# A hybrid decoder layer on one core: the recurrence's output gate goes through the Strassen pass of the mixer gates, masked copies and scans are merged, and on-chip rows are padded to 4352 bytes

## The chip, the core and the metric

The kernel runs on one core of a Trainium2 chip. A core has a matrix engine (PE, with its weight loads listed as PEld), a vector engine (DVE), a scalar engine (ACT), a general engine (POOL), and SP, whose queue issues most of the DMA transfers. Each engine works through its own queue in order, and waits on semaphores for the others. Data lives in SBUF, where a tile has 128 partitions and a row of bytes in each, and matrix products are accumulated in PSUM, which has eight banks of 512 float32 columns per partition. The metric is the device time of one execution in microseconds (us). Lower is better.

## What is computed

One layer (DEPTH is 1) on 1024 tokens of width 1024, with 16 learned meta tokens in front, so 1040 positions:

```python
u = rmsnorm(h, mix_norm_pre[l])
proj = u @ w_in[l]
q, f_logit, i_in, g_out, v_pool, gate_a, gate_b = jnp.split(proj, cuts, axis=-1)
a = hgrn2(q, f_logit, i_in, g_out, lbs[l], hgrn_out_norm[l])
p = multiscale_pool(v_pool, pool_proj[l], pool_scale[l])
z = (jax.nn.sigmoid(gate_a.astype(jnp.float32)) * (a @ w_branch_hgrn[l])
     + jax.nn.sigmoid(gate_b.astype(jnp.float32)) * (p @ w_branch_pool[l]))
h = h + rmsnorm(z @ w_out[l], mix_norm_post[l])
...
# in hgrn2: a gated recurrence over chunks with 4 heads of 128, then
o = o * lax.rsqrt(jnp.mean(o * o, axis=-1, keepdims=True) + EPS)
o = o.reshape(bsz, L, HGRN_WIDTH) * out_gain.astype(jnp.float32)
return o * jax.nn.sigmoid(g.astype(jnp.float32))
...
# in a chunk of the recurrence
b = jnp.cumsum(lf, axis=2)
scores = jnp.einsum('bhtk,bhtsk,bhsk->bhts', q, decay, k)     # causal, decay = exp(b_t - b_s)
```

After it comes a gated MLP of width 2816 with a causal convolution of three taps on the gate. Columns of `w_in`: q, f, i and the output gate g are 512 wide each (four blocks of 128, one for each head), the pooled values 512, the mixer gates a and b 1024 each.

## The kernel before, in words

Every float32 product is made of three matmuls of a rounded type: an operand is split into a high part and the rest (`act.copy` makes hi, a subtraction makes lo), and hi x hi, hi x lo and lo x hi are added up. Features lie on partitions and tokens along the rows. The normalized input is kept as `uhi` and `ulo`, eight feature blocks of 1040 columns each.

**Stages.** (1) Rows are loaded, normalized and transposed, and nine tiles of the values i are computed (L1037). Meanwhile DVE and ACT make the sums of quarters of u (t1 to t4, `gate_steps`, L966) that a Strassen product needs; `SUMS_AT` says after which tile which step of them comes. (2) Two of the four output gate projections, G0 and G1, are done by `proj` (L175): 8 feature blocks, 3 chunks of 342 columns, 3 matmuls each, 72 in all. Their sigmoid is stored to DRAM (`post_g`, L779) and loaded again by the head that needs it (L750). (3) The mixer gates a and b, 16 blocks, are eight units of `Strassen` (L191), two blocks a unit: seven products (P1 to P7) of half the depth and half the tokens in place of eight. A product has 4 blocks x 3 matmuls of 512 columns, or twice as many of 258 and 256. The first EARLY = 4 units do P1 and P2, which need no sums, ahead of the rest (L1077), and leave P1 in a slot. Weights are loaded by `load_first` and `load_unit`, summed on POOL (L255 to L258), and split four products ahead (`ahead`, L211). `put_gate` (L838) adds the products, takes the sigmoid and stores the gate to DRAM. (4) The heads of the recurrence and the pooling, in the order of the string ORDER (L45): F, Q, G and PV are projections (forget gate, query, output gate, pooled values), `h` is the next step of a head (`head_steps`, L612), `c` the logarithms and the running sum of a forget gate (`chain_f`, L592), PP the pooling products, `sp` and `sa` splits, BB and BA the two branch products, `w` the preparation of MLP weights. G2 stands after the second h2, G3 before w0. G2 and G3 keep their sigmoid in a slot. (5) The output product, the MLP (Strassen again) and its down product.

**What sets the order.** In stages 1 to 3 the order on PE, ACT and DVE is written by hand (`manual_schedule`, L1002, up to the early products). In stage 4 a planner with its own costs places the instructions; PE's order follows ORDER closely. PSUM banks come from a pool of eight (`bank`, L95) and are taken in turn, so a new product waits until the tile eight banks before it has been read. SBUF tiles called slots (`slot`, L89) come from a pool of 24, of 1040 columns (4160 bytes) each. POOLED lists the operations of stage 4 that run on POOL in place of DVE.

**A head.** For six levels of block size (2 to 64), `level_in` (L623) makes decayed q and k on DVE, ACT and POOL, `level_mm` (L637) multiplies them on PE into a bank (`sl`), and `level_out` (L657) copies the wanted half of each block into the score tile `sc`: for levels under 32 by eight masked copies of 64 columns (L669), one for each chunk of 128 tokens. Diagonal blocks (`sb`) are copied by eight masked copies of 128 columns (L725). The running sum b of the logarithms is nine scans (L602), since it starts again at every chunk. Then come the transposes of k (`pt`), the states (`ds`, `st`), the output (`po`), its norm (`ms`, `rs`), and the multiplication with the sigmoid of g (L774).

## Time and profile before

| what | value |
|---|---|
| median of three runs | 1367.71 us (1365.0 to 1373.99) |
| the profiled execution | 1363.17 us, span 1361.5 us |
| mean granted PE clock | 0.997 |
| PE busy | 98% of the span |
| DVE busy | 70% |
| ACT busy | 42% |
| POOL busy | 32% |
| DMA | 236.68 MB, mean 174 GB/s |

How to read the profile. The span runs from the first to the last instruction, and busy time is what an engine spent in instructions. Matmuls are pipelined: the duration of one holds the time to fill and drain the array, so the next one starts before it ends, and the busy time of a group is the time that is covered by at least one. A row of the waits names the waiting engine and line, the one that ended the wait, and the total, the count and the longest. A row of a stretch has from:to, the length, then the busy time and the count of instructions for PE, PEld, DVE, ACT and POOL (an engine without any is left out where one tile was asked for), and at the end the granted clock, the DMA share and GB/s. A row of a timeline has the start, the time taken, the engine, the line, the operation, output and inputs, shapes and the count, and in brackets the idle time ahead of it with what ended it. A row of groups has shapes and count, then busy time and mean ns of one, then idle time before it.

### The profile page before, as it was taken

What the parts mean: (1) busy time and instruction counts of PE and PEld (TensorE: products, weight loads), DVE (VectorE), ACT (ScalarE), POOL (GpSimd) and SP (SyncE); (2) the same over time, 40 slices, a digit from 0 to 9 for tenths busy, and PEclk for the clock granted to TensorE, in tenths of its full rate; (3) what the DMA queues carried; (4) which work ended last, traced back from release to release, by engine and by line L of the source; (5) the groups of instructions that cost most, each with busy time, mean ns of one, the idle gap of its engine ahead of it and who ended that gap; (6) DMA issues with size and microseconds to landing.
All of it is one profiled execution on the core that took longest, in us unless ns stands there. A gap on an engine that the chain in (4) does not pass through costs nothing. (4 is left out here: it accounts for less than half of the span.)

```text
span 1361.5 us, 20285 instructions
## 1 busy us (share of the span) xinstructions
PE 1336.0 (98%) x7737; PEld 1181.8 (87%) x7737; DVE 952.4 (70%) x1414; ACT 565.9 (42%) x946; POOL 439.2 (32%) x326
## 2 busy tenths in 40 slices
PE   8999999999999999999999999999999999999997
PEld 7799899999999899987778888888888887888786
DVE  6754644388886768665568888888878776744557
ACT  6543333367455474225654222222222223543343
POOL 2015421237444600051021655454566742000100
PEclk9999999999999999999999999999999999999999
DMA  7134333311110158999876877756677799965624
GB/s 266 44 115 146 117 116 108 101 54 41 34 49 19 34 173 278 323 283 310 289 259 238 225 204 201 201 173 169 158 180 157 173 243 273 386 207 186 186 62 170
DMA packets 141455, 236.68 MB, mean 174 GB/s; under 512 B 9254, under 2 KB 77450, under 8 KB 141358
## 3 DMA queue, kind: packets, MB, share of 16 engines
q1 hardware_dynamic: 129294, 211.00, 46.2%
q0 software_dynamic: 12064, 24.38, 10.6%
q8 instruction: 61, 1.00, 0.3%
q14 instruction: 36, 0.29, 0.1%
HBM read 171.85 MB, written 86.53 MB: 190 GB/s over the span
## 5 line engine op out<-in xcount | busy, mean ns | idle before, releaser
L284 PE MATMUL P<-v,whi 128*128 128x512 f32 (+2 forms) x408 | 141.5, 354 | 2.1 <-ACT p L1486 1.2
L285 PE MATMUL P<-v,whi 128*128 128x512 f32 (+2 forms) x408 | 141.0, 353 | 0.0
L287 PE MATMUL P<-v,wlo 128*128 128x512 f32 (+2 forms) x424 | 135.6, 350 | 0.0
L172 PE MATMUL pd<-rot 128*128 128x512 f32 x272 | 106.0, 390 | 0.3 <-DVE rot L1413 0.3
L173 PE MATMUL pd<-rot 128*128 128x512 f32 x272 | 106.0, 390 | 0.0
L138 POOL TENSOR_TENSOR wlo<-wraw,whi 128x1024 fp32r<-128x1024 f32 (+1 forms) x19 | 45.8, 2415 | 164.6 <-ACT whi L137 94.8
L1413 DVE TENSOR_TENSOR rot<-yt,rot 128x1024 fp32r<-128x1024 f32 x33 | 41.2, 1250 | 71.6 <-ACT rot L1412 71.6
L284 PEld LDWEIGHTS P<-v,whi 128*128 128x128 f32 x408 | 76.8, 188 | 13.1 <-ACT p L1486 1.4
L229 ACT CAST whi<-wraw 128x512 fp32r<-128x512 f32 x78 | 46.1, 618 | 97.7 <-PE P L285 86.9
L285 PEld LDWEIGHTS P<-v,whi 128*128 128x128 f32 x408 | 76.9, 189 | 10.6
L287 PEld LDWEIGHTS P<-v,wlo 128*128 128x128 f32 x424 | 74.2, 188 | 11.0
L1301 POOL TENSOR_TENSOR ys<-y 128x512 f32<-128x512 f32 x22 | 35.3, 1603 | 139.6 <-issue 95.9
L230 DVE TENSOR_TENSOR wlo<-wraw,whi 128x512 fp32r<-128x512 f32 x74 | 65.4, 905 | 19.9 <-ACT whi L229 19.9
L171 PE MATMUL pd<-rot 128*128 128x512 f32 x272 | 72.8, 391 | 2.1 <-ACT rot L1412 1.2
L255 POOL TENSOR_TENSOR swa<-wraw,wraw 128x512 f32<-128x512 f32 x28 | 44.5, 1589 | 90.7 <-DMA wraw<-in_w_in_dram 60.7
L1412 ACT CAST rot<-yt 128x1024 fp32r<-128x1024 f32 x33 | 34.6, 1051 | 90.1 <-PE pd L172 90.1
L229 ACT CAST whi<-swa 128x512 fp32r<-128x512 f32 x56 | 33.4, 618 | 88.0 <-PE P L285 79.3
L137 ACT CAST whi<-wraw 128x1024 fp32r<-128x1024 f32 (+1 forms) x28 | 26.4, 943 | 100.3 <-PE ppv L185 19.6
L1345 DVE SCALAR_TENSOR_TENSOR y<-g,par,y 128x1024 f32<-128x1024 f32 x44 | 64.3, 1462 | 0.8
L171 PEld LDWEIGHTS pd<-rot 128*128 128x128 f32 x272 | 50.9, 188 | 13.7 <-ACT rot L1412 2.0
L229 ACT CAST whi<-swb 128x512 fp32r<-128x512 f32 x56 | 33.4, 619 | 67.2 <-PE P L285 63.1
L172 PEld LDWEIGHTS pd<-rot 128*128 128x128 f32 x272 | 51.1, 188 | 11.3 <-DVE rot L1413 0.7
(387 smaller groups left out, 4187.2 us busy)
## 6 DMA issues: line engine op xcount, KB each, us to landing
wraw<-in_w_in_dram SPq DMA_DIRECT2D x36, 512.0 KB
yt<-ysum SPq DMA_DIRECT2D x33, 512.0 KB
wraw<-in_ffn_w_gate_dram SPq DMA_DIRECT2D x26, 512.0 KB
wraw<-in_w_out_dram SPq DMA_DIRECT2D x24, 512.0 KB
wraw<-in_ffn_w_up_dram SPq DMA_DIRECT2D x22, 512.0 KB
wsum<-in_ffn_w_down_dram SPq DMA_DIRECT2D x22, 512.0 KB
ysum<-ys SPq DMA_DIRECT2D x11, 768.0 KB
sa<-sscr SPq DMA_DIRECT2D x16, 513.0 KB
```

Of the source, the lines that this page charges most:

```text
L138: eng.tensor_tensor(lo, raw, rr(hi), ALU.subtract)
L171: pe.matmul(ps, ahi, bhi, start=first, stop=False)
L172: pe.matmul(ps, ahi, blo, start=False, stop=False)
L173: pe.matmul(ps, alo, bhi, start=False, stop=last)
L229: act.copy(hi, src)
L230: (pool_e if 4 <= i < 2 * self.early else dve).tensor_tensor(lo, src, rr(hi), ALU.subtract)
L255: pool_e.tensor_tensor(s1, a21, a22, ALU.add)
L284: pe.matmul(d, whi[:, k, :], xh[:, c : c + w], start=(k == 0 and onto is None), stop=False, **go)
L285: pe.matmul(d, whi[:, k, :], xl[:, c : c + w], start=False, stop=False, **go)
L287: pe.matmul(x[:, o : o + w], wlo[:, k, :], xh[:, c : c + w], start=False, stop=(k == 3), **go)
L1345: dve.scalar_tensor_tensor(a, g[:, j : j + SEQ], cvw[:, j, m : m + 1], a, ALU.mult, ALU.add)
L1413: dve.tensor_tensor(lo, src, rr(hi), ALU.subtract)
```

## The change

- The projections G are no longer done by `proj`. The four blocks of g become two more units of the gates' Strassen object (ten units in place of eight), so all four sigmoids are stored by `put_gate` and every head loads its own. G2 and G3 leave ORDER, and the code of G0, G1 and `post_g` goes.
- P1 and P2 are done early for eight units in place of four. The sums' steps are placed after tiles 5 to 8 and then after single early products. The first loads of weights are placed anew.
- `level_out` copies a level (below 32) with one masked copy of 512 columns, its mask broadcast over the chunks. The diagonal blocks take two of 512 in place of eight of 128.
- The nine scans of a head become one over 1040 columns, which multiplies the running value by a tile `keep_on` (0 at the start of each chunk, else 1) and adds. The tile is made on POOL and holds one slot.
- Slots and feature rows are 1088 columns (4352 bytes). The features begin at column 48 of their row, and the MLP's quarters use rows of 544 columns. There are 26 slots. To make room, the scratch of software-issued DMA is set to 2048 bytes, `junk` becomes a slot, and the pool of small tiles is opened after that of the slots.

```diff
-EARLY_G = 2
-SUMS_AT = {5: (2,), 6: (2, 1), 8: (3,), 9: (1, 3), 10: (1, 4), 11: (4, 0), 12: (0, 0)}
-FM_SLOTS = 24
+EARLY_G = 8
+SUMS_AT = {5: (2,), 6: (2, 1), 8: (3,), 9: (1, 3), 10: (1,), 11: (4,), 12: (4,), 13: (0,), 14: (0,), 15: (0,)}
+FM_SLOTS = 26
+LP = 1088
+U0 = LP - L
...
-        return stage["fm", "p"].tile([P, n], dtype, tag="fm", name=nm(name), padded_shape=[P, L])
+        return stage["fm", "p"].tile([P, n], dtype, tag="fm", name=nm(name), padded_shape=[P, LP])
...
-        for t0, rows in row_tiles:
-            dve.tensor_tensor_scan(b[:, t0 : t0 + rows], f[:, t0 : t0 + rows], f[:, t0 : t0 + rows],
-                                   0.0, ALU.add, ALU.bypass)
+        dve.tensor_tensor_scan(b, keep_on, f, 0.0, ALU.mult, ALU.add)
...
-            m3 = masks[lv].rearrange("p (b h) -> p b h", h=lv)
-            for c in range(NCH):
-                dve.copy_predicated(o4[:, c], m3, p4[:, c])
+            m4 = masks[lv].rearrange("p (o b h) -> p o b h", o=1, h=lv).to_broadcast([P, NCH, nb, lv])
+            dve.copy_predicated(o4, m4, p4)
...
-            for i in range(4):
-                c = 4 * j + i
-                dve.copy_predicated(sc[:, c * P : (c + 1) * P], mbase, ps[:, i * P : (i + 1) * P])
+            dve.copy_predicated(sc[:, j * 512 : (j + 1) * 512].rearrange("p (c t) -> p c t", c=4),
+                                mbase.rearrange("p (o t) -> p o t", o=1).to_broadcast([P, 4, P]),
+                                ps.rearrange("p (c t) -> p c t", c=4))
...
-        if h < EARLY_G:
-            sgs[h] = slot(TQ, name="sg")
-            nc.sync.dma_start(sgs[h], sgd[h])
+        sg = slot(TQ, name="sg")
+        nc.sync.dma_start(sg, sd[2 * KD + h])
...
-    gates = Strassen([(WIN, c + 2 * P * j) for c in (CA, CB) for j in range(KD // 2)], range(KD), EARLY, gq,
+    gate_units = [(WIN, c + 2 * P * j) for c, n in ((CA, KD), (CB, KD), (CG, HEADS)) for j in range(n // 2)]
+    gates = Strassen(gate_units, range(len(gate_units)), EARLY_G, gq,
                      lambda u: True, put_gate, lambda u, i: None)
...
-        for e in range(0, EARLY, 2):
+        at = len(vtiles)
+        for e in range(0, EARLY_G, 2):
+            for i in (e + 3, e + 4):
+                if i < EARLY_G:
+                    gates.load_first(i)
             p = gates.start_pair(e)
             for f in [f[i] for i in range(2) for f in p]:
                 f()
-                for j in SUMS_AT.get(13, ()) if e == 0 else ():
+                for j in SUMS_AT.get(at, ()):
                     next(sums[j], None)
+                at += 1
...
-            fq[q] = [t[:, i * 4 * n : (i + 1) * 4 * n].rearrange("p (k t) -> p k t", k=4)]
+            fq[q] = [t[:, i, :, :n] if n == HT else t[:, i, :, :].rearrange("p k t -> p (k t)")[:, : 4 * n].rearrange("p (k t) -> p k t", k=4)]
...
-    nc = _bacc.Bacc("TRN2", target_bir_lowering=False, num_devices=1)
+    nc = _bacc.Bacc("TRN2", target_bir_lowering=False, num_devices=1, dynamic_dma_scratch_size=2048)
```

More of the change, by code (lines that the diff above doesn't have):

```diff
@@ L43 @@
 AHEAD = 3
-ORDER = ("F0 c0 Q0 h0 F1 h0 c1 Q1 h0 h1 F2 h1 c2 h0 Q2 h1 h2 G2 h0 h1 h2 h0 F3 h0 h2 c3 PV0 h1 h2 h1 Q3 h3 h1 h3 h1 "
-         "PV1 h3 sp0 PV2 h2 h3 sa1 sp1 sp2 PP0 h2 PV3 h2 h3 sp3 PP1 h0 G3 w0 h3 PP2 h3 PP3 w1 BB0 w4 h2 BB1 w4 BB2 "
+ORDER = ("F0 c0 Q0 h0 F1 h0 c1 Q1 h0 h1 F2 h1 c2 h0 Q2 h1 h2 h0 h1 h2 h0 F3 h0 h2 c3 PV0 h1 h2 h1 Q3 h3 h1 h3 h1 "
+         "PV1 h3 sp0 PV2 h2 h3 sa1 sp1 sp2 PP0 h2 PV3 h2 h3 sp3 PP1 h0 w0 h3 PP2 h3 PP3 w1 BB0 w4 h2 BB1 w4 BB2 "
          "w4 sa2 BB3 w5 h3 BB4 w5 BB5 w5 sa0 sa3 BA0 w5 BA1 w2 BB6 w3 BA2 BB7 BA3 BA4 BA5 BA6 BA7")
@@ L68, in trunk_kernel @@
     wst = ctx.enter_context(tc.tile_pool(name="wst", bufs=3))
-    sm = ctx.enter_context(tc.tile_pool(name="sm", bufs=4))
     PSUM = bass.MemoryType.PSUM
@@ L89, in slot, with ubig @@
     def slot(n, dtype=F32, name="s"):
-        return stage["fm", "p"].tile([P, n], dtype, tag="fm", name=nm(name), padded_shape=[P, L])
-    def ubig(dtype, name, n=KD * L):
-        return upool.tile([P, n], dtype, tag="u", name=nm(name), padded_shape=[P, KD * L])
+        return stage["fm", "p"].tile([P, n], dtype, tag="fm", name=nm(name), padded_shape=[P, LP])
+    def ubig(dtype, name, n=KD * LP):
+        return upool.tile([P, n], dtype, tag="u", name=nm(name), padded_shape=[P, KD * LP])
     def bank(name="ps"):
@@ L114, in trunk_kernel @@
     open_pool("fm", FM_SLOTS)
+    stage["sm"] = ExitStack()
+    sm = stage["sm"].enter_context(tc.tile_pool(name="sm", bufs=4))
     open_pool("ps", 8, PSUM)
@@ L413, in trunk_kernel @@
     uhi_f, ulo_f = ubig(F32R, "uhi"), ubig(F32R, "ulo")
-    uhi = uhi_f.rearrange("p (k t) -> p k t", k=KD)
-    ulo = ulo_f.rearrange("p (k t) -> p k t", k=KD)
+    uhi, ulo = (u.rearrange("p (k t) -> p k t", k=KD)[:, :, U0:] for u in (uhi_f, ulo_f))
     WIN = w_in[0]
@@ L569, in u_all @@
         return uhi[:, k, lo : lo + n], ulo[:, k, lo : lo + n]
-    def u_q(k, lo, n):
-        return uhi[:, k, T0 + lo : T0 + lo + n], ulo[:, k, T0 + lo : T0 + lo + n]
     def blocks(t, lo, h):
@@ L581, in eng @@
         return pool_e if op in POOLED else dve
-    sgs = {}
     def post_f(h, pf):
@@ L664, in level_out @@
                 return
+            nb = P // (2 * lv)
             o4 = sc.rearrange("p (c b two h) -> p c b two h", c=NCH, two=2, h=lv)[:, :, :, 1, :]
             p4 = ps.rearrange("p (c b h) -> p c b h", c=NCH, h=lv)
-            m3 = masks[lv].rearrange("p (b h) -> p b h", h=lv)
-            for c in range(NCH):
-                dve.copy_predicated(o4[:, c], m3, p4[:, c])
+            m4 = masks[lv].rearrange("p (o b h) -> p o b h", o=1, h=lv).to_broadcast([P, NCH, nb, lv])
+            dve.copy_predicated(o4, m4, p4)
             if pm is not None:
@@ L772, in head_steps @@
         dve.scalar_tensor_tensor(o, o, ong[:, h : h + 1], rs, ALU.mult, ALU.mult)
-        sg = sgs[h]
         eng(f"osg.{h}").tensor_tensor(o, o, sg, ALU.mult)
         heads[h] = dict(o=o)
-    sgd = dram.tile([EARLY_G, P, TQ], F32, name="gscr")
-    def post_g(h, pg):
-        sg = slot(TQ, name="sg")
-        for (lo, n), ps in zip(CH_Q, pg):
-            act.activation(sg[:, lo : lo + n], ps[:, :n], AF.Sigmoid)
-        if h < EARLY_G:
-            nc.sync.dma_start(sgd[h], sg)
-        else:
-            sgs[h] = sg
     pooled, pin = {}, {}
@@ L834, in trunk_kernel @@
     sas, sbs, z = {}, {}, {}
-    sd = dram.tile([2 * KD, P, TQ], F32, name="sscr")
+    sd = dram.tile([2 * KD + HEADS, P, TQ], F32, name="sscr")
     def put_gate(u, i, h, a, b, c=None):
@@ L869, in job @@
             return (wblock(WIN, 0, KD, CQ + i * P, P), KD, u_all, CH_ALL, lambda r: post_q(i, r))
-        if kind == "G":
-            return (wblock(WIN, 0, KD, CG + i * P, P), KD, u_q, CH_Q, lambda r: post_g(i, r))
         if kind == "PV":
@@ L1052, in trunk_kernel @@
                 sums = [gate_steps(d) for d in ds]
+            if i == len(vtiles) - 2:
+                gates.load_first(0)
+                gates.load_first(1)
             if i == len(vtiles) - 1:
-                gl = Loader([job("G", h)[:2] + (P,) for h in range(EARLY_G)])
+                gates.ahead(4)
+                gates.load_first(2)
             for j in SUMS_AT.get(i, ()):
@@ L1057, in trunk_kernel @@
             v_out(ps, vtiles[i][0])
-        gates.load_first(0)
-        gates.load_first(1)
-        gates.ahead(2)
-        for h in range(EARLY_G):
-            src, n_k, xs, chunks, post = job("G", h)
-            r = proj(None, 0, n_k, xs, chunks, ws=gl.next(), name="pg")
-            for j in SUMS_AT.get(9 + 2 * h, ()):
-                next(sums[j], None)
-            post(r)
-            if h == 0:
-                dve.tensor_tensor(vmeta[:NM], vm_hl[:NM], vm_low[:NM], ALU.add)
-                gates.load_first(2)
-                gates.ahead(4)
-            for j in SUMS_AT.get(10 + 2 * h, ()):
-                next(sums[j], None)
+        dve.tensor_tensor(vmeta[:NM], vm_hl[:NM], vm_low[:NM], ALU.add)
         close_pool("ps")
         open_pool("pf", 4, PSUM)
-        gates.load_first(3)
-        for e in range(0, EARLY, 2):
+        at = len(vtiles)
[3 more added lines that the diff above has]
+                    gates.load_first(i)
             p = gates.start_pair(e)
@@ L1099, in split_z @@
         return zh, zl
+    keep_on = slot(L, name="keep_on")
+    pool_e.memset(keep_on, 1.0)
+    pool_e.memset(keep_on[:, NM:].rearrange("p (c t) -> p c t", t=P)[:, :, :1], 0.0)
     z0 = []
@@ L1135, in trunk_kernel @@
     if TRUNC:
-        close_pool("ps", "fm")
+        close_pool("ps", "sm", "fm")
         return
@@ L1145, in trunk_kernel @@
     for n, name, names in ((HT, "v1", ("b11h", "b11l", "b21h", "b21l")), (HN, "v2", ("b22h", "b22l", "t1h", "t1l"))):
-        t = ubig(F32R, name, 16 * n)
+        t = ubig(F32R, name).rearrange("p (i k t) -> p i k t", i=4, k=4)
         for i, q in enumerate(names):
-            fq[q] = [t[:, i * 4 * n : (i + 1) * 4 * n].rearrange("p (k t) -> p k t", k=4)]
+            fq[q] = [t[:, i, :, :n] if n == HT else t[:, i, :, :].rearrange("p k t -> p (k t)")[:, : 4 * n].rearrange("p (k t) -> p k t", k=4)]
     def add_quarters(*names):
@@ L1571, in trunk_kernel @@
     hrow = {}
-    junk = const.tile([P, 512], F32, name="junk4")
+    junk = slot(512, name="junk4")
     def load_h(t):
@@ L1649, in trunk_kernel @@
         finish(t, c11[t], c12[t])
-    close_pool("ps", "fm")
+    close_pool("ps", "sm", "fm")
 _INS = ["x", "meta_tokens", "mix_norm_pre", "mix_norm_post", "w_in", "hgrn_lower_bounds", "hgrn_out_norm",
```

## The prediction

> **What bounds the kernel now.** I read the page first, then the list of PE's waits, then busy time by stretches, and last the timelines of the engines around the four G projections.

> ```profile
> span 1361.5 us, 20285 instructions
> PE 1336.0 (98%) x7737; PEld 1181.8 (87%) x7737; DVE 952.4 (70%) x1414; ACT 565.9 (42%) x946; POOL 439.2 (32%) x326
> ```

> PE leaves 25.5 us of the span idle, so time falls only where PE gets less to do, and only if PE then finds its next operands ready. The second half of that sentence is what this change turns on. The longest wait:

> ```profile
> engine line waited for: us in total, times, longest us
> PE ppv L184 <- ACT st L735: 2.5, 1, 2.5
> ```

> **G as Strassen units, work alone.** PE's busy time for the tile of the G projections (G0 and G1, then G2, then G3), and for the products of the eight gate units:

> ```profile
> 66.00:91.00 25.00, 22.78 (x144) 22.68 (x144) 2.24 (x6) 1.00 0.41 116
> 334.00:347.00 13.00, 11.57 (x72) 11.31 (x72) 0.00 (x0) 1.00 0.17 51
> 477.00:490.00 13.00, 11.73 (x72) 11.38 (x72) 0.00 (x0) 1.00 0.14 42
> 90.00:249.00 159.00, 158.57 (x1056) 145.74 (x1056) 37.80 (x55) 4.69 (x8) 1.00 0.37 118
> ```

> One G is 11.4 us (22.78 / 2; the other two rows hold the latency of a first or last matmul as well). One unit, which makes two blocks, is 158.57 / 8 = 19.8 us. Four G are 45.6, two units 39.6: 6.0 us less PE work. But it is not taken out where it is put in. Between the V tiles and the first full unit, G0 and G1 go (-22.8) and one unit's worth comes (+19.8): -3.0. The second unit, +19.8, replaces G2 and G3, which stand among the head steps. The stretch from 90 to 249 us shows no wait of PE worth naming, with the same loads, splits, sigmoids and stores for each unit, so I cost these at PE time alone for ten units.

> More P1/P2 products early (sixteen in place of eight) also means more to evict while DVE still adds the quarter sums:

> ```profile
> 70.00:85.00 15.00, 15.00 (x98) 15.00 (x96) 13.18 (x30) 8.96 (x23) 0.00 (x0) 1.00 0.40 106
> ```

> DVE is 88% busy there. Under the new SUMS_AT, the copy of the second P1 on ACT and the first P2 addition on DVE are queued behind sum steps, and PE waits for them once its four PSUM pairs are full, that is four products (of 19.8 / 7 = 2.8 us) later. The remaining idle DVE time and that lead should cover it: I take 0, between 0 and 3 us (one product). Eight first loads in place of four take the place of the G loads; the DMA share in the row is 0.40.

> **What G2 covers.** Busy time of PE, PEld, DVE, ACT and POOL around G2, then DVE's own order:

> ```profile
> 330.00:340.00 10.00, 10.00 (x75) 9.91 (x74) 9.96 (x25) 9.23 (x15) 5.84 (x3) 1.00 0.21 54
> 340.00:350.00 10.00, 9.42 (x67) 9.11 (x66) 10.00 (x14) 5.23 (x9) 10.00 (x5) 1.00 0.18 52
> 350.00:360.00 10.00, 9.27 (x110) 8.50 (x110) 9.92 (x21) 6.73 (x11) 1.83 (x2) 1.00 0.18 61
> ```

> ```profile
> 318.15 1.67 DVE L593 TENSOR_SCALAR f<-f,oml,lb 128x1040 f32<-128x1040 f32 x1 [0.73 <-ACT f L588]
> ...
> 320.41 1.13 DVE L669 COPY_PREDICATED sc<-mask,sl 128x64 f32<-128x64 uint8 x8
> ...
> 329.83 1.24 DVE L600 TENSOR_TENSOR f<-f,f 128x1040 f32<-128x1040 f32 x1 [1.49 <-ACT f L599]
> 331.11 2.72 DVE L602 TENSOR_TENSOR_SCAN b<-f 128x16 f32<-128x16 f32 x9
> ...
> 337.31 1.15 DVE L669 COPY_PREDICATED sc<-mask,sl 128x64 f32<-128x64 uint8 x8
> ...
> 346.97 1.13 DVE L669 COPY_PREDICATED sc<-mask,sl 128x64 f32<-128x64 uint8 x8
> ...
> 358.40 0.68 DVE L663 COPY sc<-sl 64x512 f32<-64x512 f32 x1
> ```

> DVE works without a gap from 329.8 to 359.1, and before that waits only for ACT's logarithms and for the sigmoids of F2. What PE waits for when G2 is over:

> ```profile
> 348.28 2.05 PE L722 MATMUL sb<-q,kk 128*128 128x128 f32 x16 [0.58 <-POOL kk L705]
> 359.14 0.42 PE L184 MATMUL pf<-uhi,whi 128*128 128x348 f32 x1 [0.49 <-DVE sc L663]
> ```

> So F3 starts at 359.1 because DVE's copy at 358.40 empties its bank, not because PE is late. Taking G2 away frees 11.4 us of PE, but F3 comes only as much earlier as DVE does. That is the price of the next item.

> **Merged copies and scans.** Mean duration by shape, DVE:

> ```profile
> L669 DVE COPY_PREDICATED sc<-mask,sl 128x64 f32<-128x64 uint8 x128 | 19.6, 250 | 9.6 <-PE sl L649 9.5
> L725 DVE COPY_PREDICATED sc<-mbase,sb 128x128 f32<-128x128 uint8 x32 | 7.0, 297 | 9.9 <-PE sb L722 9.9
> L602 DVE TENSOR_TENSOR_SCAN b<-f 128x128 f32<-128x128 f32 x32 | 12.6, 469 | 0.0
> L602 DVE TENSOR_TENSOR_SCAN b<-f 128x16 f32<-128x16 f32 x4 | 0.8, 192 | 0.1
> ```

> Copies: 64 more columns cost 47 ns, so a copy of 512 is about 297 + 384 x 0.73 = 0.58 us, by the busy columns (153 and 219 ns each, 1.03 ns a column) 219 + 384 x 1.03 = 0.61. I take 0.65; eight small ones in a row take 1.13 to 1.15. That is 0.5 a level, 16 levels in all: 8 us, and 4 x (7.0 / 4 - 1.3) = 1.8 for the diagonal blocks. A broadcast mask could cost more than a plain one; no row shows it. Scans: (469 - 192) / 112 = 2.5 ns an element, so 1040 elements cost 2.6 us against 2.72 for nine; with the busy column (12.6 / 32 = 394 and 192 ns, 1.8 ns) it is 2.1. I take 2.3, 0.4 less per head. The new scan multiplies and adds where the old one only adds; if that doubled it, DVE would lose 2.7 us a head. In the chain above, from 318 to 359, three level copies (1.5), a diagonal (0.4) and a scan (0.4) shrink: F3 starts 2.3 us earlier if DVE keeps its order. A planner that no longer counts on G2 can pull the copy of L663 ahead of work for other heads, at most to the full 11.4. I take 5.0, nearer to the DVE rows: 6.4 of G2's 11.4 us become waiting.

> **What G3 covers.** PE before and after G3, DVE meanwhile:

> ```profile
> 476.03 1.89 PE L769 MATMUL ms<-rs,onesm 128*128 128x342 f32 x6
> 489.16 0.48 PE L734 MATMUL ds<-vmeta,ktm 16*128 16x128 f32 x2
> 497.38 0.40 PE L184 MATMUL pbb<-phi,whi 128*128 128x342 f32 x1
> ```

> ```profile
> 457.44 3.48 DVE L138 TENSOR_TENSOR wlo<-wraw,whi 128x1024 fp32r<-128x1024 f32 x1
> ...
> 482.72 1.22 DVE L822 TENSOR_TENSOR pll<-s,plh 128x1026 fp32r<-128x1026 f32 x1
> ...
> 485.00 1.53 DVE L829 SCALAR_TENSOR_TENSOR plo<-ppp,par,phi 128x342 fp32r<-128x342 f32 x3
> ```

> DVE has room here. Without G3, ds, PP2 and po could run from 477.5, but PP3 needs the split that ends at 483.9, and a PSUM bank may hang on the eviction that ends at 486.5. The pieces from 489.2 to 497.4 last 8.2 us; starting at 477.5 they would end at 485.7, and held by the eviction, with 4 us of PP3 and po behind it, near 490.5. So BB0 comes 7 to 11.4 us earlier; I take 9.0. The row at 457.44 is G3's weight split, ahead of the DVE chain that ends in the wait of 2.5 us above: that wait should go (-2.5). Two more reloads of gates on SP's queue, and six more stores, wait for nothing late; the DMA share near G2 and G3 is 0.14 to 0.21.

> **Rows of 4352 bytes.** 4352 is 17 x 256, 4160 is not a multiple of 256, so tiles in slots now start alike. PE's means for 512 columns, operands in a big tile against operands in slots:

> ```profile
> L172 PE MATMUL pd<-rot 128*128 128x512 f32 x272 | 106.0, 390 | 0.3 <-DVE rot L1413 0.3
> L287 PE MATMUL P<-t3h,wlo 128*128 128x512 f32 x120 | 47.5, 396 | 0.0
> ```

> 6 ns at most. Of the 512-column matmuls some 660 have operands that become aligned (t3 360, b22 and t1 of the gates 192, the kept y 108): 0 to 4 us, I take -2.0. [...] The 2048 bytes of scratch for software DMA, two memsets on POOL for keep_on, junk as a slot and the moved pool: 0, since POOL is idle 68% of the span.

> **The clock.** After a wait of 2.0 us, PE ran at half its clock:

> ```profile
> 690.37 0.32 PE L1198 MATMUL pt<-ident,un 114*128 114x114 f32 x1 [2.01 <-ACT tt L1215]
> ```

> ```profile
> 692.00:693.00 1.00, 1.00 (x4) 0.77 (x3) 0.92 (x4) 0.52 (x3) 0.43 (x1) 0.50 0.11 45
> 693.00:694.00 1.00, 1.00 (x3) 0.73 (x3) 0.72 (x2) 1.00 (x3) 1.00 (x2) 0.50 0.00 0
> ```

> A wait of 6.4 us at G2's place is three times as long. From these rows I add one such dip, about 3.4 us at half speed: +1.7 (0 to 3.4). [...]

> **Sum.** -3.0 + 19.8 - 5.0 - 9.0 - 2.5 - 2.0 + 1.7 = 0.0 us. The profiled execution took 1363.17 us (span 1361.5 and 1.7 around it), 4.5 under the median of the three runs, 1367.71 (1365.0 to 1373.99). So I forecast 1367.7 as a median: no change.

> **Rivals.** (1) The cover isn't missed: the order of DVE's work is planned anew, and the lost PE work is lost in full. -3.0 + 19.8 - 22.8 - 2.5 - 2.0 = -10.5, and with the 2.0 us wait and dip at 690 gone too (3.7) -14.2: 1353 to 1357. For it: DVE loses some 12 us and G2's and G3's splits. Against it: DVE without a gap from 329.8 to 359.1. (2) Slower: the head steps take as long without G2 and G3 as with them. Then neither gives anything back: -3.0 + 19.8 - 2.0, and a dip for each hole (3.4): +18.2, 1386. For it: both ends of G2's stretch wait for DVE and POOL. Against it: DVE at G3 is half idle. It decides from the point where both together give back under about 7 us. (3) The alignment does nothing: +2, inside the forecast's own range.

> **How the numbers follow.** Forecast 0.48, its own range 1360 to 1376 (G2 2.3 to 8, G3 7 to 11.4, the early products up to +3). Faster rival 0.30, two thirds of it over 1%. Slower rival 0.22, most of it over 1%, as its price lies between +8 and +18. Range 1352 to 1383. About 1% (13.7 us) is what a measurement of this kernel can tell from no change: faster 0.22, same 0.58, slower 0.20.

> **What would show it.** No gap of PE between the V tiles and unit 0, and ten units at 19.8 us: the first terms. F3's first matmul behind a wait for L663 or POOL's kk: G2's cover. A gap between ms and the first BB0: G3's. One masked copy a level at 0.65 us, one scan at 2.3. A granted clock under 1.00 near the gaps. If head steps run with PE busy throughout, I am wrong toward faster; if the early products stall by several us or a merged scan takes over 4 us, toward slower.

## The result, and the profile after

The changed kernel takes 1386.65 us (median of four runs, 1384.93 to 1387.14), the kernel before, in the same series, 1367.19 us: a ratio of 1.0138 (95% interval 1.0102 to 1.0173), 19.5 us slower. The profiled execution took 1386.82 us, with a span of 1385.1 us and a mean granted clock of 0.984 (before 0.997). The forecast was 1367.7 in a range of 1352 to 1383; the slower rival, "the head steps take as long without G2 and G3 as with them", had 1386.

The head of the page, and the longest of PE's waits:

```profile
span 1385.1 us, 20125 instructions
...
PE 1342.9 (97%) x7713; PEld 1186.7 (86%) x7713; DVE 970.0 (70%) x1262; ACT 566.7 (41%) x951; POOL 453.5 (33%) x344
```

```profile
PE sl L644 <- DVE d L629: 6.2, 2, 6.1
PE ppp L187 <- ACT st L730: 3.6, 1, 3.6
PE pm L175 <- DMA wlo<-wlos: 2.6, 2, 1.4
PE pt L707 <- DVE kd L689: 2.2, 1, 2.2
```

The wait of 2.5 us of ppv for st is gone, as forecast, and a longer one stands first: PE's level products sl wait 6.1 us for one multiplication on DVE. PE is also busy 6.9 us longer than before, although it has less to do. That is the first hint of the clock: the same matmuls take longer at half speed (16 of the sl 3.68 us in place of 2.00, below).

Where the 23.6 us of span come from is read off the first matmul of each group (F0 is the first `pf`, and so on). It is more than the 19.5 us between the medians, because the profiled execution of the kernel before (1363.17 us) was 4.0 us under the median of its series. Lengths in us; "ms" is the norm's matmul in front of G3's place, counted to its end:

| stretch | before | after | difference | forecast |
|---|---|---|---|---|
| start to F0 | 248.8 | 264.4 | +15.6 | +16.8, less alignment |
| F0 to Q2 | 71.0 | 71.4 | +0.4 | 0 |
| Q2 to PV0 (G2's place, F3) | 58.8 | 67.5 | +8.7 | -5.0, clock +1.7 |
| PV0 to the end of ms | 99.3 | 96.7 | -2.6 | -2.5 (the wait) |
| end of ms to BB0 (G3's place) | 19.5 | 14.2 | -5.3 | -9.0 |
| BB0 to the first pm | 96.2 | 103.2 | +7.0 | 0 |
| pm to the end | 767.9 | 767.7 | -0.2 | alignment |
| sum | 1361.5 | 1385.1 | +23.6 | 0.0 |

So the first part of the working held, and the two places of G2 and G3 did not. Busy time by stretches at G2's place (PE, PEld, DVE, ACT, POOL, then the granted clock):

```profile
350.00:360.00 10.00, 5.84 (x37) 5.25 (x36) 9.96 (x7) 4.76 (x10) 7.46 (x4) 0.83 0.02 7
360.00:370.00 10.00, 3.25 (x50) 2.82 (x50) 10.00 (x16) 7.35 (x13) 3.57 (x3) 0.57 0.16 53
370.00:380.00 10.00, 8.42 (x39) 7.92 (x40) 9.82 (x14) 1.22 (x3) 0.00 (x0) 0.50 0.01 2
380.00:390.00 10.00, 10.00 (x52) 10.00 (x53) 2.88 (x8) 0.19 (x1) 0.00 (x0) 0.74 0.00 1
```

PE is idle for 12.5 of the first 30 us while DVE is busy for 29.8 of them, and the clock is at half from 361.4 to 385.3 us by the trace's clock record. From 380 on it is the other way round: PE is busy, and DVE has 2.9 us of work in ten. PE's timeline of the place:

```profile
353.46 1.06 PE L707 MATMUL pt<-ident,kd 128*128 128x128 f32 x8 [2.19 <-DVE kd L689]
...
362.36 3.16 PE L640 MATMUL sl<-d 128*32 128x32 f32 x48 [1.96 <-POOL d L629]
371.58 3.68 PE L644 MATMUL sl<-d 128*128 128x64 f32 x16 [6.06 <-DVE d L629]
...
379.82 3.35 PE L736 MATMUL ds<-vh,kt 128*128 128x128 f32 x14
382.83 0.64 PE L187 MATMUL pf<-uhi,whi 128*128 128x348 f32 x1
```

A group of 16 sl takes 3.68 us here, 2.00 at full clock (at 349.28).

### The profile page after: what moved, and what is told of

The parts are those of the page before. It is cut to its first block, busy times and chain, and to the rows that moved or that the text cites. A ratio compares the mean times of both kernels' runs of the same rounds, so it can differ in the third digit from the quotient of the medians.

```text
span 1385.1 us, 20125 instructions
## 1 busy us (share of the span) xinstructions
PE 1342.9 (97%) x7713; PEld 1186.7 (86%) x7713; DVE 970.0 (70%) x1262; ACT 566.7 (41%) x951; POOL 453.5 (33%) x344
## 3 DMA queue, kind: packets, MB, share of 16 engines
q0 software_dynamic: 12064, 24.38, 10.4%
## 5 line engine op out<-in xcount | busy, mean ns | idle before, releaser
L287 PE MATMUL P<-v,whi 128*128 128x512 f32 (+2 forms) x408 | 141.9, 356 | 2.2 <-DVE p L346 1.2
L287 PEld LDWEIGHTS P<-v,whi 128*128 128x128 f32 x408 | 77.2, 189 | 13.1 <-DVE p L346 1.6
L232 ACT CAST whi<-wraw 128x512 fp32r<-128x512 f32 x84 | 49.8, 617 | 94.2 <-PE P L288 76.7
L290 PEld LDWEIGHTS P<-v,wlo 128*128 128x128 f32 x424 | 74.4, 189 | 11.3
L140 ACT CAST whi<-wraw 128x1024 fp32r<-128x1024 f32 (+1 forms) x24 | 22.2, 924 | 104.2 <-PE pf L188 24.4
L174 PEld LDWEIGHTS pd<-rot 128*128 128x128 f32 x272 | 51.0, 188 | 13.4 <-ACT rot L1390 1.6
L288 PE MATMUL P<-t4l,whi 128*128 128x258 f32 (+1 forms) x212 | 61.3, 306 | 0.0
```

The source lines that it names most:

```text
L174: pe.matmul(ps, ahi, bhi, start=first, stop=False)
L232: act.copy(hi, src)
L287: pe.matmul(d, whi[:, k, :], xh[:, c : c + w], start=(k == 0 and onto is None), stop=False, **go)
L288: pe.matmul(d, whi[:, k, :], xl[:, c : c + w], start=False, stop=False, **go)
L290: pe.matmul(x[:, o : o + w], wlo[:, k, :], xh[:, c : c + w], start=False, stop=(k == 3), **go)
```

## Experiments

Every kernel ran against the kernel before in its own series, whose median was between 1364.7 and 1367.2 us; ratios to it compare best across series.

| kernel | us | ratio to before | 95% interval |
|---|---|---|---|
| changed kernel | 1386.65 | 1.0138 | 1.0102 to 1.0173 |
| g23_projections | 1360.11 | 0.9963 | 0.9950 to 0.9976 |
| after_filler | 1374.58 | 1.0068 | 1.0053 to 1.0083 |
| filler_g2 | 1373.25 | 1.0051 | 1.0036 to 1.0066 |
| filler_half | 1370.51 | 1.0037 | 1.0020 to 1.0054 |
| filler_late | 1379.97 | 1.0107 | 1.0087 to 1.0126 |
| order_pv | 1388.06 | 1.0159 | 1.0143 to 1.0175 |
| order_f3b | 1373.80 | 1.0062 | 1.0043 to 1.0082 |
| order_w0 | 1382.57 | 1.0128 | 1.0112 to 1.0145 |
| ms_late | 1385.57 | 1.0161 | 1.0138 to 1.0183 |
| ms_late_f3b_w0 | 1371.89 | 1.0061 | 1.0038 to 1.0085 |
| pv_swap | 1390.81 | 1.0182 | 1.0164 to 1.0200 |
| pv_swap_f3b | 1384.11 | 1.0127 | 1.0112 to 1.0142 |
| pv_swap_f3b_w0 | 1380.77 | 1.0105 | 1.0082 to 1.0128 |
| g23_pv_swap | 1378.56 | 1.0088 | 1.0055 to 1.0121 |
| before_merged | 1367.71 | 1.0017 | 1.0007 to 1.0027 |
| before_rows | 1364.13 | 0.9990 | 0.9979 to 1.0002 |
| after_unmerged | 1383.30 | 1.0122 | 1.0106 to 1.0139 |
| g23_unmerged | 1363.70 | 0.9989 | 0.9976 to 1.0003 |

### Is it the cover? One unit only: g23_projections

```diff
-    ... for c, n in ((CA, KD), (CB, KD), (CG, HEADS)) ...
+    ... for c, n in ((CA, KD), (CB, KD), (CG, 2)) ...
-ORDER = "... Q2 h1 h2 h0 h1 ... PP1 h0 w0 h3 ..."
+ORDER = "... Q2 h1 h2 G2 h0 h1 ... PP1 h0 G3 w0 h3 ..."
```

> The changed kernel, but G2 and G3 are projections again at their old places, and only G0 and G1 are a (ninth) unit. Theory A (cover): the loss of 19.5 us lies in the second unit (+19.8) that got nothing back, since G2's and G3's PE work covered DVE and kept the clock up. Then this kernel is 0 to 6 us under the kernel before (-3.0 of the first unit, 0 to -2.5 for the wait at ppv), F3 starts 11 to 13 us after where the second unit is missing, and no half clock of over 7 us shows in the head stage. Theory B (the merged operations, the padded rows or the new plan themselves make the head stage longer): the head stage from the first pf to the first pm stays within 5 us of the changed kernel's 353 us, and the kernel is slower than the kernel before by 8 us or more.

0.9963 of the kernel before, so 5.0 us faster. The clock is 1.00 throughout the head stage, Q2 to PV0 takes 57.6 us and BB0 to pm 96.6. Theory A holds, and B falls: the merged operations and the rows are the changed kernel's own here. Against this kernel the changed one is 23.9 us slower by the ratios (0.0175 x 1367), more than the second unit's 19.8 us: on balance nothing of them came back. This is also the version that beats both kernels.

### Work that nobody needs makes it faster: after_filler, filler_g2, filler_half

```diff
+        if kind == "x":
+            idle_banks = [bank("jk") for _ in CH_Q]
+            for k in range((8, 8)[i - 2]):
+                for (lo, n), ps in zip(CH_Q, idle_banks):
+                    for part in (uhi, ulo, uhi):
+                        pe.matmul(ps[:, :n], uhi[:, k, T0 : T0 + P], part[:, k, T0 + lo : T0 + lo + n], start=True, stop=True)
+            continue
```

In ORDER, x2 stands behind the second h2 (G2's old place) and x3 ahead of w0 (G3's). filler_g2 has (8, 0) in place of (8, 8), filler_half (4, 4).

> The changed kernel with 72 matmuls of 342 columns added at each of G2's and G3's old places, on data that is there already and into banks that nobody reads; they compute nothing that is used. 22.8 us of PE work is added and nothing else. Theory A1 (PE idled there anyway, and the half clock that follows the idling costs time of its own): the added work is more than free, the clock stays at 1.00 around 350 to 390 us, and the time is 3 to 15 us under the changed kernel. Theory A2 (the chain on DVE and POOL alone sets the time there, the clock costs nothing): within 3 us of the changed kernel. Theory B (PE was busy with needed work and lost time by something else): slower than the changed kernel by 10 to 23 us.

> As after_filler, with the unused 72 matmuls at G2's old place only. Theory A1 (idling at G2's place is followed by a half clock that costs time of its own): F3 starts near 374 us in place of 382.8, as in after_filler, G3's place stays as in the changed kernel, and the time is 1376 to 1380 us, 7 to 10 under the changed kernel's 1386.65. Theory C (the gain of after_filler came at G3's place): 1384 to 1390.

> As after_filler, with 36 unused matmuls (5.7 us) at each of the two places. If the chain on DVE, POOL and ACT alone sets when F3 can start once the clock holds, F3 starts at 373 to 376 us, the clock stays at 1.00 and the time is 1371 to 1376. If 5.7 us are too little to hold the clock, half clock shows between 355 and 390 us, F3 comes at 377 to 383 and the time is 1378 to 1387. If every us of added work counts in full, as with an engine that is busy anyway: 1397.

With 22.8 us of useless PE work added, the kernel is 9.6 us faster by the ratios ((1.0138 - 1.0068) x 1367). All of it comes at G2's place: filler_g2 gains 11.9, its F3 starts at 374.1. With half the filler F3 starts at 374.2, and the kernel gains 13.8. So A1 holds in where F3 starts, and theory C falls. The time of filler_g2, 1373.25 us, is under the 1376 to 1380 that I gave for A1: besides the 9.9 us at G2's place, BB0 to pm takes 100.1 us in place of 103.2. The filler does one thing besides keeping PE busy: like G2 it takes three of the eight PSUM banks in turn, and that was not tested apart. order_f3b below takes none, and G2's place gets as short there.

One reading of mine needs care. In filler_half the clock did fall:

```profile
350.00:360.00 10.00, 7.99 (x58) 7.73 (x56) 9.97 (x7) 4.73 (x10) 7.47 (x4) 1.00 0.02 6
360.00:370.00 10.00, 8.44 (x83) 7.72 (x83) 10.00 (x15) 7.14 (x13) 2.54 (x3) 0.66 0.08 23
370.00:380.00 10.00, 10.00 (x74) 9.74 (x74) 9.96 (x16) 1.73 (x4) 1.46 (x1) 1.00 0.09 32
```

and F3 came only 0.1 us later. This half clock cost nothing: with the full filler PE stands 0.7 us in front of ds for DVE's copy of sc, with half of it PE arrives later and does not wait there.

```profile
373.40 0.91 PE L736 MATMUL ds<-vh,kt 128*128 128x128 f32 x6 [0.71 <-DVE sc L658]
```

So something else than the clock differs, too, and it is seen in DVE's timeline, first of the changed kernel, then of after_filler:

```profile
363.99 1.30 DVE L684 TENSOR_TENSOR kd<-b 128x16 f32<-128x16 f32 x2
365.21 0.69 DVE L629 TENSOR_TENSOR d<-d,kk 128x520 f32<-128x520 f32 x1
...
368.95 1.96 DVE L690 TENSOR_TENSOR qs<-qs,q 128x1040 f32<-128x1040 f32 x1
370.83 0.69 DVE L629 TENSOR_TENSOR d<-d,kk 128x520 f32<-128x520 f32 x1
```

```profile
364.14 0.68 DVE L629 TENSOR_TENSOR d<-d,kk 128x520 f32<-128x520 f32 x1
364.75 0.69 DVE L628 TENSOR_TENSOR d<-d,q 128x520 f32<-128x520 f32 x1
365.36 0.69 DVE L629 TENSOR_TENSOR d<-d,kk 128x520 f32<-128x520 f32 x1
365.97 1.29 DVE L684 TENSOR_TENSOR kd<-b 128x16 f32<-128x16 f32 x2
```

The second L629 (head 2) is what PE's next 32 level products wait for. With the filler it is done at 366.0. Without it PE does pt and sb of head 0 9 us sooner (353.5 in place of 362.4) and the level products of head 1 3 us sooner (362.4 in place of 365.3). The diagonal copies of head 0 and kd and qs of head 1 then stand ahead of L629 on DVE, and it ends at 371.5. That the plan puts them ahead because they are ready sooner fits both timelines; the planner's own reckoning is on no record.

### Clock or order: filler_late

```diff
-ORDER = "... Q2 h1 h2 h0 h1 h2 h0 F3 ..."
+ORDER = "... Q2 h1 h2 h0 h1 x2 h2 h0 F3 ..."     # x2 with range(4); no x3
```

> 36 unused matmuls (5.7 us) at G2's place, as in filler_half, but placed just ahead of the matmuls sl that wait 6.1 us for DVE's multiplication L629 in the changed kernel, and none at G3's place. DVE's order stays that of the changed kernel up to F3. It splits the 8.7 us by which F3 came earlier in filler_g2. If the half clock is all of it, F3 starts at 374 to 375 us. If the half clock is the part that the changed kernel's own timeline gives (from sl at 371.6 to F3 at 382.8 in 11.2 us, of which half is lost), sl still starts near 371.6 and F3 at 377 us; time 1379 to 1382. If the order on DVE is all of it, F3 stays at 382 to 383, time near 1386.

The orders of DVE, ACT and POOL up to F3 are the changed kernel's, instruction for instruction. PE's timeline:

```profile
372.40 1.90 PE L644 MATMUL sl<-d 128*128 128x64 f32 x16
...
377.10 0.48 PE L729 MATMUL ds<-vmeta,ktm 16*128 16x128 f32 x2 [0.60 <-DVE sc L658]
377.51 2.95 PE L736 MATMUL ds<-vh,kt 128*128 128x128 f32 x14
380.11 0.64 PE L187 MATMUL pf<-uhi,whi 128*128 128x348 f32 x1
```

The level products run at full clock (1.90), but ds then waits for DVE and falls into one more half clock (378.0 to 381.4). F3 starts at 380.1, not at the 377 I expected, and Q2 to PV0 takes 64.0 us. So of the 9.9 us between 67.5 and the filler's 57.6, 3.5 are shown to be the clock's (at least, as ds here still ran at half), and the other 6.4 go only where the order on DVE or on PE changes as well. The forecast by the timeline alone gave the clock 5.6, as it left out what would be late next.

### Real work as cover: order_pv and order_f3b

```diff
 order_pv
-"... Q2 h1 h2 h0 h1 h2 h0 F3 h0 h2 c3 PV0 ... PV1 h3 sp0 PV2 h2 h3 ..."
+"... Q2 h1 h2 PV0 h0 h1 h2 h0 F3 h0 h2 c3 PV1 ... PV2 h3 sp0 h2 h3 ..."
 order_f3b
-"... Q2 h1 h2 h0 h1 h2 h0 F3 h0 h2 c3 ..."
+"... Q2 h1 h2 h0 h1 F3 h2 h0 h0 h2 c3 ..."
```

> The changed kernel with real work at G2's old place: PV0 stands there, PV1 where PV0 stood, PV2 where PV1 stood, and PV2's own place is left empty. If the loss is the missing cover, F3 starts at 373 to 376 us with the clock at 1.00, and the hole moves to where PV2 was, around 455 us, where DVE is busy 8.5 of 20 us and can give time back: 1366 to 1378. If the hole costs as much wherever it is: 1383 to 1390.

> The changed kernel with F3 moved three head steps earlier (behind h0 h1 in place of h0 h1 h2 h0), nothing else. F3's 11.6 us then cover the wait of 6.1 us for L629. If DVE can give way (it is busy 3.7 of 20 us right after F3 in the changed kernel), the head stage gets back 8 to 13 us: 1374 to 1379. If DVE and POOL set the time in any order, the wait reappears behind F3 and the time stays at 1383 to 1390.

order_pv is a miss: with PV0 at G2's place F3 still starts only at 381.4, since DVE's L629 comes late all the same:

```profile
370.23 3.64 PE L644 MATMUL sl<-d 128*128 128x64 f32 x16 [2.79 <-DVE d L629]
...
378.44 3.36 PE L736 MATMUL ds<-vh,kt 128*128 128x128 f32 x14
381.45 0.64 PE L187 MATMUL pf<-uhi,whi 128*128 128x348 f32 x1
```

and PV2's empty place brought a second half clock (465.7 to 479.4). But DVE's order was not at fault here. Up to the second L629 it is that of after_filler, and two multiplications took 2.88 and 2.41 us where the same ones take 0.7 in after_filler:

```profile
363.66 2.88 DVE L628 TENSOR_TENSOR d<-d,q 128x520 f32<-128x520 f32 x1
366.45 2.41 DVE L629 TENSOR_TENSOR d<-d,kk 128x520 f32<-128x520 f32 x1
```

That is 3.9 us, about what L629 is late by. POOL was busy with two operations of 2.4 us each from 363.6 to 368.3; whether that slowed them was not tested. So order_pv says little for or against cover. In order_f3b F3 itself stands in the wait for L629:

```profile
362.50 3.16 PE L640 MATMUL sl<-d 128*32 128x32 f32 x48 [1.97 <-POOL d L629]
365.58 0.66 PE L187 MATMUL pf<-uhi,whi 128*128 128x348 f32 x1
...
378.42 1.89 PE L644 MATMUL sl<-d 128*128 128x64 f32 x16
```

and the kernel gains 10.4 us by the ratios, with no added work. Q2 to PV0 takes 57.5 us. With 11.4 us of filler it is 57.6, with 5.7 us 57.6, with F3 earlier and no filler 57.5, and with the real G2 in g23_projections 57.6. Before it was 58.8. So taking G2's 11.4 us of PE work away, or putting it back, changed this stretch by next to nothing, and in these orders the place gave back some 1.3 us, and not 5.0.

The equal lengths do not show one fixed chain behind them. In after_filler and g23_projections PE is idle for only 0.7 and 0.6 us of the stretch, so there PE is full as well. In order_f3b PE is idle for 7.2 us, 6.3 of it in four waits for DVE and POOL up to 362.5, and after F3 it is DVE that waits for PE:

```profile
380.35 1.32 DVE L664 COPY_PREDICATED sc<-mask,sl 128x512 f32<-128x512 uint8 x1 [4.31 <-PE sl L644]
```

And ms_late_f3b_w0 below, with the same order up to PV0, took 56.4 us.

### G3's place and the branch products: order_w0, ms_late, pv_swap

```diff
 order_w0
-"... PP1 h0 w0 h3 PP2 h3 PP3 w1 BB0 w4 ..."
+"... PP1 h0 h3 PP2 h3 PP3 w0 w1 BB0 w4 ..."
 ms_late
-"... PP1 h0 w0 h3 PP2 h3 PP3 w1 BB0 w4 ..."
+"... PP1 w0 h3 PP2 h3 PP3 w1 BB0 h0 w4 ..."
 pv_swap: PV0 and PV3, sp0 and sp3, PP0 and PP3 exchanged in ORDER
```

> The changed kernel with w0 (one preparation of MLP weights, on ACT and DVE) moved from G3's place to behind PP3. If it was w0's work on ACT that kept the eviction of ds (the wait of 3.6 us of PP2 for ACT's copy st), the wait at 503 us goes or falls under 1.5 us, the half clock behind it with it, and the time is 1380 to 1384. If the chain of the norm (rs) and the splits sets it, 1385 to 1389.

> The changed kernel with PV0 and PV3, sp0 and sp3, PP0 and PP3 exchanged in the order, nothing else. PV3 has four additions on POOL behind it (8.3 us in the changed kernel's trace, 490.1 to 498.5), PV0 one (some 2 us); the last split, and with it the last PP and the first BB, hang on the last PV. If that chain sets the time at G3's place, from ms (ends at 500.0) to the first BB at 514.2, that stretch of 14.2 us falls by 3 to 6 us, and the time is 1378 to 1384. If ACT's chain of the norm (two table loads, rs, then the splits) sets it, it stays within 1.5 us and the time is 1385 to 1389.

> The changed kernel with one step of head 0 (its norm: ms, two table loads, rs, on ACT 4.7 us) moved from in front of w0 to behind the first BB, nothing else. If ACT's chain of the norm, which stands ahead of the eviction st and of the splits, sets the time at G3's place, the wait of 3.6 us of PP2 for st goes, the stretch from the end of PP1 (498.2) to the first BB (514.2), 16.0 us, falls by 4 to 7 us, and the time is 1377 to 1384. If the chain behind PV3 or DVE sets it, the stretch falls by no more than the 1.9 us of ms itself and the time is 1384 to 1389.

At G3's place ACT's own order in the changed kernel is:

```profile
499.18 1.28 ACT L764 ACT_TABLE_LOAD   x1
500.48 1.42 ACT L764 ACTIVATE rs<-ms,eps_t 128x342 f32<-128x342 f32 x3
501.91 1.28 ACT L765 ACT_TABLE_LOAD   x1
503.21 1.06 ACT L765 ACTIVATE rs<-rs 128x1026 f32<-128x1026 f32 x1
...
506.41 0.27 ACT L730 COPY st<-ds 128x128 f32<-128x128 f32 x1
```

The copy st takes 0.27 us and stands 6 us behind the ds that it reads (done at 500.4), behind the norm's two table loads. order_w0 left the wait of 3.6 us as it was: w0 is not the reason. Its time, 1382.57 us, lies in the range that I had given for w0 as the reason, but for another one. In ms_late the norm is gone from here, and the stretch from the end of PP1 to BB0 falls from 16.0 to 11.7 us, as ACT's chain had it. The wait is still 2.8 us, as the plan leaves st behind other copies:

```profile
PE ppp L187 <- ACT st L730: 2.8, 1, 2.8
...
PE pbb L187 <- ACT whi L150: 2.2, 1, 2.2
```

The gain went behind BB0: BB0 to pm takes 106.8 us in place of 103.2. The branch products now wait 2.2 us for weights that ACT splits late (the second line), and the 1.9 us of ms stand there too. The time does not move (1.0161, its interval overlaps the changed kernel's). order_w0 in turn took 3.1 us off the branch products in its trace (100.1), though the intervals of 1.0128 and 1.0138 overlap. From the end of ms to pm it is 117.4 us in the changed kernel, 115.7 before with G3's 11.4 us of PE work inside, 110.9 with 5.7 us of filler (filler_half). What G3's place gives back, the branch products pay back. The likely reason is that ACT and DVE have the same work to do and start it under less cover; no run shows it by itself. In filler_half PE has no gap from 490 to 520 us and the clock stays at 1.00, and the two stretches together are 6.5 us shorter than in the changed kernel. In the changed kernel PE's loss there is idle time and a half clock again:

```profile
500.00:510.00 10.00, 5.42 (x32) 4.70 (x33) 7.26 (x11) 9.15 (x17) 0.00 (x0) 0.91 0.43 149
510.00:520.00 10.00, 10.00 (x57) 10.00 (x57) 6.53 (x14) 2.77 (x4) 0.00 (x0) 0.75 0.66 218
520.00:530.00 10.00, 8.35 (x36) 6.34 (x35) 5.24 (x9) 8.70 (x13) 0.00 (x0) 0.83 0.83 286
```

6.2 us idle, and 5.1 lost to a clock at half for 6.8 and 3.4 us: together 11.3, about what G3's matmuls had taken.

pv_swap falls as a theory: ms to BB0 took 15.9 us, not 8 to 11. Its companions say no more than that the exchange is bad by itself, and g23_pv_swap lies outside both of its forecasts:

> pv_swap with F3 moved as in order_f3b (1373.8 us, 12.9 under the changed kernel). If the two places are independent: pv_swap's gain more, 1366 to 1371 if pv_swap gains 3 to 8 us, else 1373 to 1376. If the plan shifts the gain elsewhere: 1377 or more.

> pv_swap_f3b with w0 behind the last PP as in order_w0 (which gained 4.1 us, in the stretch from the first BB to the first pm). If the three are independent: 3 to 5 us under pv_swap_f3b, 1362 to 1367, and at the kernel before or under it. If not: within 2 us of pv_swap_f3b.

> g23_projections with the same exchange. There G3's matmuls cover the place, so by the theory that the chain costs only where its cover is gone this is within 2 us of g23_projections (5.2 us under the kernel before): 3 to 7 us under the kernel before. If the exchange by itself is worth something everywhere, 8 us or more under the kernel before.

With all cover in place (g23_pv_swap) the exchange costs 17 us against g23_projections (0.0125 x 1366), so it can't serve as a test of G3's place. Why it costs that much was not followed up.

### All of it together: ms_late_f3b_w0

Its order has the edits of order_f3b, order_w0 and ms_late.

> ms_late with F3 three head steps earlier (order_f3b, 12.9 us) and w0 behind PP3 (order_w0, 4.1 us): all four changes of order that speak for themselves, with all four G in the Strassen units. If they add up: 1386.7 - 12.9 - 4.1 and 3 to 9 for ms_late, 1361 to 1367, no slower than the kernel before. If BB, which then covers the norm, loses what the places gain: 1368 to 1375.

1.0061: no better than order_f3b alone (1.0062). The branch products lost what the two places gained (BB0 to pm 105.5 us in place of order_f3b's 100.6). No version with all four G in the Strassen pass reached the kernel before; the nearest was the one with 11.4 us of useless matmuls in it.

### The other parts: before_merged, before_rows, after_unmerged, g23_unmerged

These put the merged copies and the single scan into the kernel before (before_merged), or take them out (the two others); before_rows puts in only the rows, slots and pools.

```diff
-            m3 = masks[lv].rearrange("p (b h) -> p b h", h=lv)
-            for c in range(NCH):
-                dve.copy_predicated(o4[:, c], m3, p4[:, c])
+            m4 = masks[lv].rearrange("p (o b h) -> p o b h", o=1, h=lv).to_broadcast([P, NCH, P // (2 * lv), lv])
+            dve.copy_predicated(o4, m4, p4)
...
-        for t0, rows in row_tiles:
-            dve.tensor_tensor_scan(b[:, t0 : t0 + rows], f[:, t0 : t0 + rows], f[:, t0 : t0 + rows],
-                                   0.0, ALU.add, ALU.bypass)
+        dve.tensor_tensor_scan(b, keep_on, f, 0.0, ALU.mult, ALU.add)
```

> The kernel before with only the merged masked copies and the single scan (keep_on as a constant tile, 2048 bytes of scratch). Theory A: DVE has some 11 us less to do, PE is 98% busy and mostly does not wait for it: 0 to 4 us faster than the kernel before. Theory B (a merged operation is handed on later than the first small ones were, and holds PSUM banks longer): 3 to 10 us slower.

> The kernel before with only the rows of 4352 bytes (26 slots, features from column 48, the MLP's quarters in rows of 544 columns, 2048 bytes of scratch, junk as a slot). The sum of the prediction has -2.0 us for it; by the matmuls' means of the changed kernel (t3h 389 ns in place of 393 over 360 of them, the other tiles within 1 ns) it is 1 to 2 us faster. Theory B (the rows cost time, by transfers or by where slots come free): 3 us slower or more.

> The changed kernel with eight small masked copies for a level, eight for the diagonal blocks and nine scans for a head again. DVE has some 11 us more to do. If merging helps where DVE is the limit (no gap on DVE from 316 to 380 us), F3 comes 3 to 6 us later than in the changed kernel and the time is 1389 to 1395. If merging is worth nothing or costs time, as in the kernel before (+2.4 us), 1382 to 1388.

> g23_projections (one unit for G0 and G1, rows of 4352 bytes) without the merged copies and scans. Merging cost 2.4 us in the kernel before and 3.4 in the changed one; if it does so here, this kernel is 2 to 4 us under g23_projections, that is 7 to 9 us under the kernel before. If merging helps here, it is 0 to 5 us under the kernel before.

Merging takes DVE time away, but its worth has no fixed sign: +0.17% in the kernel before, about +0.16% in the changed one (within both intervals), -0.26% with one unit. So it moves PE's waits about by 2 to 4 us either way and is not the cause of the loss. The +2.4 us of before_merged lies outside both of its forecasts. Why the sign changes stays open. With the rows alone the kernel is 1.2 us faster by the medians, with an interval of 2.9 faster to 0.3 slower: not clear of no change.

## Why the prediction was wrong, point by point

- **G0 and G1 against a unit (-3.0), a second unit (+19.8), early evictions (0).** Right. F0 comes 15.6 us later. The ten units' products are busy for 196.59 us, 19.66 a unit (158.57 / 8 = 19.82 before), so the early stretch also has 1.6 us of the alignment in it. PE waits 0.7 us at 67.45, ahead of unit 0, for the eviction of a V tile, and 0.4 us at 87.98 for an early eviction.

```profile
60.00:266.00 206.00, 196.59 (x1320) 181.71 (x1320) 48.01 (x70) 5.84 (x10) 1.00 0.41 130
```

- **Alignment (-2.0).** Right in the matmuls: 1.6 us in the gate units; the t3 matmuls went from 392 to 396 ns to 389, in g23_projections too. In the kernel's time it does not stand clear of the noise (before_rows).

```profile
L287 PE MATMUL P<-t3h,whi 128*128 128x512 f32 x128 | 49.8, 389 | 0.0
```

- **Merged copies and scans.** The sum was near, 11.0 us less on DVE in place of 11.4: 5.8 for the levels (forecast 8), 1.1 for the diagonal blocks (1.8), 4.1 for the scans (1.6). A level takes 861 ns on average in place of 650: twelve of the sixteen copies take 0.69 to 0.74 us, and the first one of each head (block size 2) 1.27 to 1.31. Why that one is longer, and what a plain mask of 512 columns would cost, no run shows.

```profile
L664 DVE COPY_PREDICATED sc<-mask,sl 128x512 f32<-128x512 uint8 x16 | 13.8, 861 | 8.6 <-PE sl L644 8.5
L598 DVE TENSOR_TENSOR_SCAN b<-keep_on,f 128x1040 f32<-128x1040 f32 x4 | 9.3, 2324 | 0.2
L718 DVE COPY_PREDICATED sc<-mbase,sb 128x512 f32<-128x512 uint8 x8 | 5.9, 736 | 8.0 <-PE sb L717 8.0
```

- **"I take 5.0 ... 6.4 of G2's 11.4 us become waiting."** This is the step that failed. From Q2 F3 came 7.7 us later in place of 5.0 sooner, and the place became 8.7 us longer. I let the plan pull the copy that F3 waits for ahead of other work, and my range (2.3 to 8) had no case in which DVE's order gets worse. It did get worse: work of heads 0 and 1 stands ahead of the multiplication that PE waits for, which ends 5.5 us later than with the filler, and PE then works at half clock (371.6 to 385.3). A better estimate was in the profile: DVE without a gap over the stretch, less what the merged operations save there, which was the 2.3 of my own DVE rows. The kernels in which the place came out best took 56.4 to 57.6 us, 1.2 to 2.4 under before.
- **The clock (+1.7, one dip of 3.4 us).** Mis-sized. The 3.4 us are the length of the dip behind the wait of 2.0 us in the profile before (first row). That a longer wait brings a dip was my estimate: the same profile has a wait of 2.5 us with the clock at 1.00 throughout (second row), and in the changed kernel both dips at G2's place begin ahead of the wait of 6.1 us (at 354.57 and 361.40; the wait is from 365.5 to 371.6). The half clock there lasted 3.4 and 23.9 us, at G3's place 6.8 and 3.4. filler_late shows at least 3.5 us of cost at G2's; at G3's it is 5.1 by the clock record, as PE is busy nearly throughout those two dips. filler_half's dip of 6.8 us, in and behind waits for DVE, cost 0.1: it is the work that nothing else holds up that pays.

```profile
691.33:694.74 3.41, 3.41 (x10) 2.46 (x9) 2.17 (x7) 2.81 (x9) 2.09 (x3) 0.50 0.19 79
460.00:470.00 10.00, 7.53 (x52) 7.00 (x51) 8.73 (x15) 1.71 (x5) 4.24 (x3) 1.00 0.21 62
```

- **G3's place (7 to 11.4, I took 9.0).** It gave back 5.3, and the branch products, which the sum had at nothing, took 7.0. I had read DVE as half idle there, and had not looked at ACT, whose norm stands ahead of the eviction of ds, nor at what ACT and DVE would carry over into BB. How much of the 7.0 is which stays open.
- **The wait of 2.5 us.** Right, that stretch is 2.6 us shorter.
- **The rivals.** The slower one was nearest, in its reason too (both ends of G2's stretch wait for DVE and POOL). I gave it 0.22. That its 1386 met the 1386.65 us so closely is luck: it had 1.7 us of clock for each place and no more, and measured were 8.7 us at G2's place, 1.7 at G3's with the branch products, and 2.6 less for the wait of ppv, which it left out. What spoke against it, DVE half idle at G3, was an average over an engine that was not the one that mattered.

## What to carry to other kernels

Where PE work is saved by moving it, the place it leaves is worth only what the other engines' work there leaves over, and that can be measured: add useless matmuls at the place, or move the next real product there, and see whether the end moves. PE work among dependent small steps paid twice here, as cover and by keeping the clock up (1.00 from Q2 to PV0 with G2 in place in g23_projections, half for 3.4 and 23.9 us without it). A planned order can get worse when an engine comes early, so look at which instruction PE waits for and what the other engine did in the 5 us before it; here one multiplication of 0.69 us was 5.5 us late.

## What the hardware showed that was not expected

At full clock the clock held over the same small matmuls in g23_projections (1.00 from Q2 to PV0), but in before_merged it fell to half behind them, although PE had no gap. The two rows are the 3.41 us of sl and the first ds, and the 3.41 us after it:

```profile
354.04:357.45 3.41, 3.41 (x30) 3.10 (x29) 3.33 (x7) 2.67 (x5) 0.00 (x0) 1.00 0.00 0
357.45:360.86 3.41, 3.41 (x16) 3.41 (x17) 3.41 (x4) 2.36 (x5) 2.80 (x1) 0.50 0.49 154
```

So a busy PE in the profile was not enough there to hold the clock. With the wide matmuls of F3 it came back 2.4 to 2.8 us after the first of them (the changed kernel, order_pv, order_f3b). 6.8 us of narrow ones in the changed kernel, 33 matmuls of 64 and 8 columns that the profile shows as a busy PE, did not bring it back:

```profile
371.64:378.46 6.82, 6.82 (x33) 6.68 (x33) 6.74 (x11) 1.15 (x2) 0.00 (x0) 0.50 0.01 2
```
